# Third mixer of a hybrid encoder layer: the centring and the first chunk's right sides move into the two visits that complete the inverses, and merged values are turned eight blocks a visit

## Chip, cores and metric

The kernel runs on one core of a Trainium2 chip. The core has five engines with their own instruction queues: TensorE (PE in the profile; its weight loads are shown as PEld), VectorE (DVE), ScalarE (ACT), GpSimd (POOL) and SyncE (SP), which here only starts DMA transfers. The metric is the device time of one execution in microseconds; the median of the runs counts.

## What is computed

One encoder layer with a sequence of 256 tokens and a width of 2048. Three mixers read one normalised projection of the input, a gate is put on each, and an output product and an MLP follow:

```python
proj = u @ w_in                                   # u: RMS norm of x
y_a = stick_breaking_attention(...)               # first mixer
y_b = forgetting_attention(...)                   # second mixer
y_c = rwkv7_time_mix(rw, ...)                     # third mixer, 16 heads of 64
m = g_a * (y_a @ w_branch_a) + g_b * (y_b @ w_branch_b) + g_c * (y_c @ w_branch_c)
x = x + rms_norm(m @ w_out)
x = x + rms_norm(jnp.square(relu(rms_norm(x) @ w_mlp_up)) @ w_mlp_down)
```

The third mixer is a recurrence over time with a 64 by 64 state for each head:

```python
sa = jnp.einsum('bhvk,bhk->bhv', state, kk_t)
state = state * w_t[:, :, None, :] - sa[..., None] * kka_t[:, :, None, :] + v_t[..., None] * k_t[:, :, None, :]
y = jnp.einsum('bhvk,bhk->bhv', state, r_t)
```

Then each head's output has its mean taken away, is divided by its deviation and scaled (a group norm), and is gated.

## The kernel before

**The stream of weights.** Nearly all of the time goes to large products of activations with weights read once from memory, each element kept as a rounded high part and a low part. `wraw` (L162) issues a DMA of 512 KB from SyncE into one of three `raw` buffers. `wsplit` (L170) makes the high part `whi` on ScalarE (L173) and the low part `wlo` on VectorE (L175), each in one of three buffers. TensorE then multiplies with both, in `gemm` (L187, matmuls at L191, L195 and L197) or in `tok` (L208, matmuls at L220 and L235). These are the large matmuls in what follows, of 512 or 256 columns. A step of `tok` is one such weight tile: eight large matmuls with `whi`, then four with `wlo`.

**The mixers beside it.** The mixers are a generator. `tick` (L137) is called at fixed places of the stream, twice a step of the stream as a rule; it adds a credit of 0.88 (`SHARE`) times a weight and runs pieces of the generator as long as there is credit and no hold. A piece ends with a `yield`: a plain number costs that much credit, and `("stage", cost, hold)` also holds the generator back for that many ticks. So small matmuls of the mixers come between the large ones in groups; such a group is called a visit here. A list `hooks` is served at each tick too, one entry a tick.

**What sets the order.** From L436 on, only TensorE's instructions stand in the order in which the code writes them (`manual_schedule(engines={PE})`). VectorE's and ScalarE's order is made by a list scheduler with its own estimate of when operands are ready. A change that only moves matmuls therefore also moves instructions of VectorE and ScalarE.

**The third mixer, one half of the heads at a time** (`rwkv_half`, run for half 0 and half 1). Time is cut in four chunks of 64. For each of four pairs of heads, matmuls at L836 make the products of keys within the chunks, and VectorE masks them into SC. Then comes the part that the change touches:

- Centring: 16 matmuls at L857 take the mean over a head away from the values `v`, by a constant matrix "cen", into two PSUM tiles; 8 ScalarE copies (L862) put them into four tiles Xt. This is a visit of its own, ahead of the inverse.
- The inverse: VectorE transposes SC to U (L876) and inverts 64 triangular blocks of 32 by 32 in 31 steps (L881 and L883, tiles tp and Ti). Then it transposes the inverses Ti to TW (L888) and back into SC (L893).
- Two visits complete the inverses of the 64 by 64 blocks: 32 matmuls at L898 with TW, copied back to TW by ScalarE (L900), and 32 at L905, copied to SC (L908).
- For each chunk c: right sides at L928 (from chunk 1 on also L924), copied by ScalarE to `rh` (L932); the solution at L937, copied to Xt (L941, L943); then the outputs and the next state (L949, L955, L958).

**Merged values.** After each gate and branch product, the sum `m` of the gated branches, 256 tokens by 512 columns, is turned by `turn`: each call makes four transposes of 128 by 128 on TensorE (L1112) and splits the result into two tiles `pk` (ScalarE L259, VectorE L260). Six of these calls, for the first three groups of columns, are hooks during the fourth group's branch product of the third mixer.

Of the kernel before, what the change touches and what calls it, by code (L numbers as in the profile page):

```python
# [11 lines left out]
F32 = mybir.dt.float32  # L12
F32R = mybir.dt.float32r
AF = mybir.ActivationFunctionType
ALU = mybir.AluOpType
AX = mybir.AxisListType
# [36 lines left out]
def hybrid_block(ctx, tc, xt, x, gains, params, consts, lora, gup, wst, out):  # L53
    nc = tc.nc
    V, A, G, PE = nc.vector, nc.scalar, nc.gpsimd, nc.tensor
# [10 lines left out]
    def nm(s):  # L66
        uid[0] += 1
        return f"{s}_{uid[0]}"
# [4 lines left out]
    def mps():  # L73
        return pm.tile([128, 512], F32, tag="mps", name=nm("mps"), bufs=4)
# [11 lines left out]
    def C(name, r=slice(0, 128), lo=0, hi=None):  # L86
        c0, w = CC[name]
        hi = w if hi is None else hi
        if name == "ident":
            return ident[r, lo:hi]  # L90
        if c0 < NR + 128:
            return cr[r, c0 - 128 + lo:c0 - 128 + hi].bitcast(F32)
        return con[r, c0 - 128 - NR + lo:c0 - 128 - NR + hi]
# [13 lines left out]
    done = {}  # L107
# [6 lines left out]
    each, hooks = [], []  # L114
# [610 lines left out]
    def rwkv_half(hf):  # L725
# [26 lines left out]
        pss = []  # L752
# [97 lines left out]
            V.tensor_tensor(bon[p], psb[:, 0:T], v, ALU.mult)  # L850
            yield ("stage", 1.9, 3.5 if i == 0 else 2.0)

        pss = [mps(), mps()]
        for i, p in enumerate(PR):
            for cc in range(4):
                o = 256 * (i % 2) + 128 * (cc // 2)
                PE.matmul(pss[i // 2][64 * (cc % 2):64 * (cc % 2) + 64, o:o + 128], done[f"v{p}"][:, cc * 64:cc * 64 + 64],  # L857
                          C("cen"), start=True, stop=True)
        for i, p in enumerate(PR):
            Xt[p] = rp.tile([128, 4, 128], F32, tag="AX", name=nm("Xt"), bufs=5)  # L860
            for b in range(2):
                A.activation(Xt[p][64:128, b:4:2, :],  # L862
                             pss[i // 2][64 * b:64 * b + 64, 256 * (i % 2):256 * (i % 2) + 256]
                             .rearrange("p (c t) -> p c t", c=2), AF.Copy)
        yield ("stage", 0.2, 1)

        U = rp.tile([64, 32, 32], F32, tag="b6", name=nm("U"), bufs=1)
        Ti = rp.tile([64, 32, 32], F32, tag="Ti", name=nm("Ti"), bufs=1)
        tp = rp.tile([64, T], F32, tag="kkr", name=nm("tp"), bufs=1)
# [27 lines left out]
        for j in range(32):  # L897
            PE.matmul(ps[32 * (j % 4):32 * (j % 4) + 32, j // 4 * 32:j // 4 * 32 + 32], SC[0:32, j, 32:64],  # L898
                      TW[0:32, j, :], start=True, stop=True)
        for g in range(4):  # L900
            A.activation(TW[32:64, g:32:4, :], ps[32 * g:32 * g + 32, 0:256].rearrange("p (a b) -> p a b", a=8), AF.Copy)
        yield ("stage", 0.2, 3)
        ps = mps()
        for j in range(32):
            PE.matmul(ps[32 * (j % 4):32 * (j % 4) + 32, j // 4 * 32:j // 4 * 32 + 32], TW[32:64, j, :],  # L905
                      SC[32:64, j, 32:64], start=True, stop=True)
        for g in range(4):
            A.activation(SC[0:32, g:32:4, 32:64], ps[32 * g:32 * g + 32, 0:256].rearrange("p (a b) -> p a b", a=8),  # L908
                         AF.Copy)
        yield ("stage", 0.2, 2)  # L910


        Pb = rp.tile([128, 4, 128], F32, tag="Pb", name=nm("Pb"), bufs=1)
        G.memset(Pb, 0.0)
        y = {p: g1() for p in PR}
        HC = (slice(0, 64), slice(64, 128))
        for c in range(4):
            sls = [[i * 8 + h * 4 + c for h in range(2)] for i in range(4)]
            co = [slice(64 * i, 64 * i + 64) for i in range(4)]
            psr = mps()  # L920
            if c:
                for i, p in enumerate(PR):
                    for hc in HC:
                        PE.matmul(psr[hc, co[i]], Bt[p][:, c, 0:64], Pb[:, i, hc], start=i == 0, stop=False,  # L924
                                  skip_group_check=True)
            for i, p in enumerate(PR):
                for h, hc in enumerate(HC):
                    PE.matmul(psr[hc, co[i]], SC[64:128, sls[i][h], 0:64], Xt[p][64:128, c, hc],  # L928
                              start=c == 0 and i == 0, stop=True, skip_group_check=True)
            rhs = rp.tile([64, 4, 128], F32, tag="rh", name=nm("rh"), bufs=1)  # L930
            for hc in HC:
                A.activation(rhs[:, :, hc], psr[hc, 0:T].rearrange("p (a b) -> p a b", a=4), AF.Copy)  # L932
            yield ("stage", 0.9, 1)
            pso = [mps(), mps()]
            for i in range(4):
                for h, hc in enumerate(HC):
# [170 lines left out]
    def turn(g, j):  # L1107
        ps = mps()
        for i in range(2):
            for tt in range(2):  # L1110
                c = 256 * i + 128 * tt
                PE.transpose(ps[:, c:c + 128], ms[g][:, tt, (j + i) * 128:(j + i) * 128 + 128], C("ident"))  # L1112
        for i in range(2):
            mpk[4 * g + j + i] = pk()
            split(ps[:, T * i:T * i + T], mpk[4 * g + j + i], 0.5)

    for g in range(4):
        if g == 3:
            hooks.extend([lambda: None] * 12)
            for k in range(0, 12, 2):  # L1120
                hooks.extend([lambda k=k: turn(k // 4, k % 4), lambda: None])
        branch(ycp, thc.pop(0) if thc else gate(), ms[g], False)
    hooks.extend([lambda: None] * 4 + [lambda: turn(3, 0), lambda: None, lambda: turn(3, 2)])
    wo = tok(mpk)
# [587 lines left out]
```

## Time and profile before

| | us |
|---|---|
| median of three runs (1503.62, 1504.09, 1506.31) | 1504.09 |
| the profiled execution | 1505.64 |
| its span, first to last instruction | 1503.8 |
| TensorE busy | 1489.7 (99%) |
| TensorE weight loads busy | 1250.7 (83%) |
| VectorE busy | 1206.8 (80%) |
| ScalarE busy | 938.4 (62%) |
| GpSimd busy | 91.1 (6%) |
| mean granted TensorE clock | 0.998 |

A row of a timeline is: start, length, engine, line, operation, output and inputs by the program's tile names, their shape, and how many equal instructions in a row are put together. Where an engine stood idle ahead of it, the idle time and what ended it stand in brackets. TensorE's matmuls overlap: a row's length is from the start of its first to the modelled end of its last, so times are compared from start to start. A small matmul of the mixers shows as two in the trace: the 16 of the centring read x32, the 32 at L898 x64 and the 8 right sides of a chunk x16.

### The profile page before, as it was taken

The numbers are of one execution on the slowest core, as the hardware profiler recorded it, in microseconds if no ns is written. First come the engines' busy times: TensorE is split into PE (matmuls) and PEld (weight loads), VectorE is DVE, ScalarE is ACT, GpSimd is POOL, SyncE is SP. The second block draws the span as 40 slices with busy tenths as digits, with TensorE's granted clock in tenths as the row PEclk, the third lists the DMA queues.
The fourth block names the chain that finished last, engine by engine and source line by source line (L and its number), as shares of the span: only waits on it lengthen the run. The fifth ranks groups of instructions, "written<-read, shape, count | busy, mean of one in ns | idle before, by whom it ended". The sixth has DMA issues, their size and how long they took to land.

```text
span 1503.8 us, 22719 instructions
## 1 busy us (share of the span) xinstructions
PE 1489.7 (99%) x8384; PEld 1250.7 (83%) x8384; DVE 1206.8 (80%) x1677; ACT 938.4 (62%) x1435; POOL 91.1 (6%) x151
## 2 busy tenths in 40 slices
PE   9999999999999999999999999999999999999997
PEld 7888888887788887788888888888888888888886
DVE  7965679895688796476657788999899989999996
ACT  7665677545776445564445776776767666767663
POOL 0011003000001000000000000000000000000000
PEclk9999999999999999999999999999999999999999
DMA  8545445454445455345674768879888888889874
GB/s 284 202 150 178 151 158 169 155 182 162 157 167 173 150 192 189 135 165 195 226 243 161 261 179 256 252 223 286 243 269 239 225 279 258 249 259 261 256 216 149
DMA packets 107055, 312.19 MB, mean 208 GB/s; under 512 B 12352, under 2 KB 14400, under 8 KB 106944
## 3 DMA queue, kind: packets, MB, share of 16 engines
q1 hardware_dynamic: 96336, 279.35, 54.8%
q0 software_dynamic: 8064, 29.36, 10.5%
q10 hardware_dynamic: 2544, 2.03, 0.5%
q8 instruction: 66, 1.08, 0.3%
q14 instruction: 45, 0.37, 0.1%
HBM read 279.24 MB, written 2.10 MB: 187 GB/s over the span
## 4 chain that ended last, share of the span: by engine, by line
PE 94%; DVE 2%; ACT 1%; issue 1%; DMA 0%; SPq 0%; POOLq 0%; DVEq 0%; POOL 0%; ACTq 0%
PE gps L235 27%; PE gps L191 22%; PE gps L195 12%; PE gps L220 7%; PE mps L1430 3%; PE mps L1432 3%; PE mps L1431 3%; PE gps L1432 2%; PE gps L1430 2%; PE gps L1431 2%; PE gps L197 2%; DVE wlo L175 1%; PE mps L836 1%; PE gps L359 1%; PE gps L1219 1%
## 5 line engine op out<-in xcount | busy, mean ns | idle before, releaser
L175 DVE TENSOR_TENSOR wlo<-raw,whi 128x1024 fp32r<-128x1024 f32 x570 | 691.3, 1223 | 151.5 <-ACT whi L173 141.8
L173 ACT ACTIVATE whi<-raw 128x1024 fp32r<-128x1024 f32 x570 | 597.9, 1057 | 246.5 <-PE gps L235 71.7
L191 PE MATMUL gps<-pk,whi 128*128 128x512 f32 x1460 | 370.7, 392 | 1.0 <-ACT whi L173 0.8
L191 PEld LDWEIGHTS gps<-pk,whi 128*128 128x128 f32 x1460 | 270.6, 188 | 56.4 <-ACT whi L173 1.7
L235 PE MATMUL gps<-whi,pk 128*128 128x512 f32 x1004 | 253.5, 392 | 0.0
L195 PEld LDWEIGHTS gps<-pk,wlo 128*128 128x128 f32 x1561 | 212.8, 190 | 15.4 <-DVE wlo L175 0.5
L235 PEld LDWEIGHTS gps<-whi,pk 128*128 128x128 f32 x1004 | 186.4, 188 | 40.0 <-issue 1.0
L195 PE MATMUL gps<-pk,wlo 128*128 128x256 f32 x1561 | 218.0, 282 | 0.1
L235 PE MATMUL gps<-wlo,pk 128*128 128x512 f32 x502 | 138.1, 393 | 0.1
L235 PEld LDWEIGHTS gps<-wlo,pk 128*128 128x128 f32 x502 | 93.1, 188 | 20.0 <-DVE wlo L175 0.5
L1347 ACT ACTIVATE tmp<-gps 128x256 f32<-128x256 f32 x64 | 24.6, 385 | 105.2 <-PE gps L197 103.3
L1430 PE MATMUL mps<-whi,fm 128*128 128x512 f32 x224 | 88.6, 396 | 1.4 <-ACT whi L173 1.3
L1431 PE MATMUL mps<-whi,fm 128*128 128x512 f32 x224 | 87.7, 392 | 0.0
L1432 PE MATMUL mps<-wlo,fm 128*128 128x512 f32 x224 | 87.4, 390 | 0.0
L1410 POOL DMA_DIRECT2D raw<-raw x56 | 48.8, 872 | 571.9 <-DVE raw L1407 279.8
L1407 DVE TENSOR_TENSOR raw<-raw,raw 128x1024 f32<-128x1024 f32 x56 | 68.4, 1222 | 0.8
L1430 PE MATMUL gps<-whi,fm 128*128 128x512 f32 x168 | 65.8, 392 | 0.0
L1432 PE MATMUL gps<-wlo,fm 128*128 128x512 f32 x168 | 65.7, 391 | 0.0
L1431 PE MATMUL gps<-whi,fm 128*128 128x512 f32 x168 | 65.5, 390 | 0.0
L220 PE MATMUL gps<-whi,pk 128*128 128x512 f32 x224 | 60.8, 393 | 0.0
L1430 PEld LDWEIGHTS mps<-whi,fm 128*128 128x128 f32 x224 | 42.3, 189 | 9.7 <-ACT whi L173 3.5
L1432 PEld LDWEIGHTS mps<-wlo,fm 128*128 128x128 f32 x224 | 42.1, 188 | 9.4
(358 smaller groups left out, 1743.0 us busy)
## 6 DMA issues: line engine op xcount, KB each, us to landing
raw<-in_wst_dram SPq DMA_DIRECT2D x510, 512.0 KB, 4.3
raw<-raw POOLq DMA_DIRECT2D x56, 512.0 KB, 7.2
x<-in_xt_dram SPq DMA_DIRECT2D x8, 256.0 KB, 5.6
x<-in_x_dram SPq DMA_DIRECT2D x8, 256.0 KB, 5.5
raw<-in_wst_dram SPq DMA_DIRECT2D x6, 256.0 KB, 4.9
pk<-in_wst_dram SPq DMA_DIRECT2D x6, 256.0 KB, 5.1
g<-in_gains_dram SPq DMA_DIRECT2D x4, 256.0 KB, 5.0
pk<-in_gains_dram SPq DMA_DIRECT2D x4, 256.0 KB, 6.8
```

The costliest lines, as they stand in the source:

```text
L173: A.activation(hi, raw, AF.Copy)
L175: low = lambda: V.tensor_tensor(lo, raw, hi.bitcast(F32), ALU.subtract)
L191: PE.matmul(ps, hi[:, i * 128:i * 128 + 128], pks[i], start=first and i == 0, stop=False)
L195: PE.matmul(ps[:, 0:T], lo[:, i * 128:i * 128 + 128], pks[i][:, 0:T], start=False, stop=False)
L197: PE.matmul(ps, hi[:, (n - 1) * 128:n * 128], pks[n - 1], start=False, stop=True)
L220: PE.matmul(ps[tt], pks[k][:, c:c + 128], w[:, (k - k0) * 512:(k - k0) * 512 + 512], start=k == 0 and part == 0 and w is hl[0], stop=w is ...
L235: PE.matmul(ps[tt], pks[k][:, c:c + 128], w[:, (k - k0) * 512:(k - k0) * 512 + 512], start=k == 0 and part == 0 and w is hl[0], stop=False)
L1407: V.tensor_tensor(R[d, a], R[d, a], R[d, b], ALU.add)
L1410: G.dma_start(out=R[d, a], in_=R[d, b], accum_op=ALU.add)
L1430: PE.matmul(Q[f], a, w, start=d == d0 and i == 0, stop=False)
L1431: PE.matmul(Q[f], b, w, start=False, stop=False)
L1432: PE.matmul(Q[f], a, wl, start=False, stop=d == dn and i == 1)
```

## The change

In `rwkv_half` the centring visit ahead of the inverse is removed. Its 16 matmuls now follow the 32 at L898 in the first of the two completing visits, and its copies to Xt follow ScalarE's copies to TW, in two parts. The right sides of chunk 0 (L928 with c = 0) now follow the 32 matmuls of the second completing visit (L905), and the copy to `rh` follows the copies to SC. Holds and credits are divided anew, with the same sum of holds. The transposes of merged values in the hooks come as three entries of eight transposes, four ticks apart, in place of six entries of four, two ticks apart. No instruction is added or removed on any engine.

```diff
@@ -850,20 +850,6 @@
             V.tensor_tensor(bon[p], psb[:, 0:T], v, ALU.mult)
             yield ("stage", 1.9, 3.5 if i == 0 else 2.0)
 
-        pss = [mps(), mps()]
-        for i, p in enumerate(PR):
-            for cc in range(4):
-                o = 256 * (i % 2) + 128 * (cc // 2)
-                PE.matmul(pss[i // 2][64 * (cc % 2):64 * (cc % 2) + 64, o:o + 128], done[f"v{p}"][:, cc * 64:cc * 64 + 64],
-                          C("cen"), start=True, stop=True)
-        for i, p in enumerate(PR):
-            Xt[p] = rp.tile([128, 4, 128], F32, tag="AX", name=nm("Xt"), bufs=5)
-            for b in range(2):
-                A.activation(Xt[p][64:128, b:4:2, :],
-                             pss[i // 2][64 * b:64 * b + 64, 256 * (i % 2):256 * (i % 2) + 256]
-                             .rearrange("p (c t) -> p c t", c=2), AF.Copy)
-        yield ("stage", 0.2, 1)
-
         U = rp.tile([64, 32, 32], F32, tag="b6", name=nm("U"), bufs=1)
         Ti = rp.tile([64, 32, 32], F32, tag="Ti", name=nm("Ti"), bufs=1)
         tp = rp.tile([64, T], F32, tag="kkr", name=nm("tp"), bufs=1)
@@ -897,40 +883,60 @@
         for j in range(32):
             PE.matmul(ps[32 * (j % 4):32 * (j % 4) + 32, j // 4 * 32:j // 4 * 32 + 32], SC[0:32, j, 32:64],
                       TW[0:32, j, :], start=True, stop=True)
+        pss = [mps(), mps()]
+        for i, p in enumerate(PR):
+            for cc in range(4):
+                o = 256 * (i % 2) + 128 * (cc // 2)
+                PE.matmul(pss[i // 2][64 * (cc % 2):64 * (cc % 2) + 64, o:o + 128], done[f"v{p}"][:, cc * 64:cc * 64 + 64],
+                          C("cen"), start=True, stop=True)
         for g in range(4):
             A.activation(TW[32:64, g:32:4, :], ps[32 * g:32 * g + 32, 0:256].rearrange("p (a b) -> p a b", a=8), AF.Copy)
-        yield ("stage", 0.2, 3)
+        yield ("stage", 0.1, 1.5)
+        for i, p in enumerate(PR):
+            Xt[p] = rp.tile([128, 4, 128], F32, tag="AX", name=nm("Xt"), bufs=5)
+            if i == 2:
+                yield ("stage", 0.1, 1.5)
+            for b in range(2):
+                A.activation(Xt[p][64:128, b:4:2, :],
+                             pss[i // 2][64 * b:64 * b + 64, 256 * (i % 2):256 * (i % 2) + 256]
+                             .rearrange("p (c t) -> p c t", c=2), AF.Copy)
+        yield ("stage", 0.2, 2)
         ps = mps()
         for j in range(32):
             PE.matmul(ps[32 * (j % 4):32 * (j % 4) + 32, j // 4 * 32:j // 4 * 32 + 32], TW[32:64, j, :],
                       SC[32:64, j, 32:64], start=True, stop=True)
+        HC = (slice(0, 64), slice(64, 128))
+        co = [slice(64 * i, 64 * i + 64) for i in range(4)]
+        psr = mps()
+        for i, p in enumerate(PR):
+            for h, hc in enumerate(HC):
+                PE.matmul(psr[hc, co[i]], SC[64:128, i * 8 + h * 4, 0:64], Xt[p][64:128, 0, hc], start=i == 0,
+                          stop=True, skip_group_check=True)
         for g in range(4):
             A.activation(SC[0:32, g:32:4, 32:64], ps[32 * g:32 * g + 32, 0:256].rearrange("p (a b) -> p a b", a=8),
                          AF.Copy)
-        yield ("stage", 0.2, 2)
+        yield 0.2
 
 
         Pb = rp.tile([128, 4, 128], F32, tag="Pb", name=nm("Pb"), bufs=1)
         G.memset(Pb, 0.0)
         y = {p: g1() for p in PR}
-        HC = (slice(0, 64), slice(64, 128))
         for c in range(4):
             sls = [[i * 8 + h * 4 + c for h in range(2)] for i in range(4)]
-            co = [slice(64 * i, 64 * i + 64) for i in range(4)]
-            psr = mps()
             if c:
+                psr = mps()
                 for i, p in enumerate(PR):
                     for hc in HC:
                         PE.matmul(psr[hc, co[i]], Bt[p][:, c, 0:64], Pb[:, i, hc], start=i == 0, stop=False,
                                   skip_group_check=True)
-            for i, p in enumerate(PR):
-                for h, hc in enumerate(HC):
-                    PE.matmul(psr[hc, co[i]], SC[64:128, sls[i][h], 0:64], Xt[p][64:128, c, hc],
-                              start=c == 0 and i == 0, stop=True, skip_group_check=True)
+                for i, p in enumerate(PR):
+                    for h, hc in enumerate(HC):
+                        PE.matmul(psr[hc, co[i]], SC[64:128, sls[i][h], 0:64], Xt[p][64:128, c, hc],
+                                  start=False, stop=True, skip_group_check=True)
             rhs = rp.tile([64, 4, 128], F32, tag="rh", name=nm("rh"), bufs=1)
             for hc in HC:
                 A.activation(rhs[:, :, hc], psr[hc, 0:T].rearrange("p (a b) -> p a b", a=4), AF.Copy)
-            yield ("stage", 0.9, 1)
+            yield ("stage", 0.9, 1 if c else 2)
             pso = [mps(), mps()]
             for i in range(4):
                 for h, hc in enumerate(HC):
@@ -1117,8 +1123,8 @@
     for g in range(4):
         if g == 3:
             hooks.extend([lambda: None] * 12)
-            for k in range(0, 12, 2):
-                hooks.extend([lambda k=k: turn(k // 4, k % 4), lambda: None])
+            for k in range(3):
+                hooks.extend([lambda k=k: [turn(k, 0), turn(k, 2)]] + [lambda: None] * 3)
         branch(ycp, thc.pop(0) if thc else gate(), ms[g], False)
     hooks.extend([lambda: None] * 4 + [lambda: turn(3, 0), lambda: None, lambda: turn(3, 2)])
     wo = tok(mpk)
```

TensorE's order around the first completing visit of the first half, before (the L898 matmuls read TW; `whi` and `wlo` are the parts of a weight tile, with its number):

```order
L235 MATMUL gps_3470<-wlo_3533,pk_332 128x512
L235 MATMUL gps_3471<-wlo_3533,pk_332 128x512
L235 MATMUL gps_3470<-wlo_3533,pk_333 128x512
L235 MATMUL gps_3471<-wlo_3533,pk_333 128x512
L898 MATMUL mps_3566<-TW_3447,SC_2240 32x32 x32
L235 MATMUL gps_3470<-whi_3550,pk_334 128x512 x2
```

and after, where these matmuls are at L884 and the centring is at L890:

```order
L235 MATMUL gps_3440<-wlo_3503,pk_332 128x512
L235 MATMUL gps_3441<-wlo_3503,pk_332 128x512
L884 MATMUL mps_3534<-TW_3405,SC_2240 32x32 x32
L890 MATMUL mps_3567<-con,g_448_2349 64x128 x4
L890 MATMUL mps_3567<-con,g_468_2427 64x128 x4
L890 MATMUL mps_3568<-con,g_480_2486 64x128 x4
L890 MATMUL mps_3568<-con,g_497_2564 64x128 x4
L235 MATMUL gps_3440<-wlo_3503,pk_333 128x512
```

The visit stands two large matmuls earlier in the stream, and the centring follows in it. The second completing visit and the right sides of chunk 0 were two visits, at L905 and L928, with one step of the stream between them; after, they are one:

```order
L220 MATMUL gps_3441<-wlo_3619,pk_338 128x512
L220 MATMUL gps_3441<-wlo_3619,pk_339 128x512
L906 MATMUL mps_3659<-SC_2240,TW_3405 32x32 x32
L913 MATMUL mps_3692<-Xt_3607,SC_2240 64x64 x2
L913 MATMUL mps_3692<-Xt_3610,SC_2240 64x64 x2
L913 MATMUL mps_3692<-Xt_3613,SC_2240 64x64 x2
L913 MATMUL mps_3692<-Xt_3634,SC_2240 64x64 x2
L235 MATMUL gps_3716<-whi_3641,pk_1346 128x512 x2
```

It stands where the right sides stood, twelve large matmuls behind the place of L905. VectorE's order at the end of the inverse of the first half, before:

```order
L881 TENSOR_TENSOR tp_3042<-U_3040,Ti_3041 64x31
L883 TENSOR_TENSOR Ti_3041<-Ti_3041,tp_3042 64x31
L175 TENSOR_TENSOR wlo_3533<-raw_3530,whi_3532 128x1024
L888 STREAM_TRANSPOSE TW_3447<-Ti_3041 32x16x32 x2
L893 STREAM_TRANSPOSE SC_2240<-Ti_3041 32x16x32 x2
L175 TENSOR_TENSOR wlo_3551<-raw_3548,whi_3550 128x1024
```

and after (L881, L883, L888 and L893 are now L867, L869, L874 and L879):

```order
L867 TENSOR_TENSOR tp_3002<-U_3000,Ti_3001 64x31
L869 TENSOR_TENSOR Ti_3001<-Ti_3001,tp_3002 64x31
L175 TENSOR_TENSOR wlo_3521<-raw_3518,whi_3520 128x1024
L874 STREAM_TRANSPOSE TW_3405<-Ti_3001 32x16x32 x2
L879 STREAM_TRANSPOSE SC_2240<-Ti_3001 32x16x32 x2
L175 TENSOR_TENSOR wlo_3594<-raw_3591,whi_3593 128x1024
```

The rows look alike, but the `wlo` ahead of TW is now that of the step behind the visit (before it was that of the step just ahead of it): all are one step further on. In the second half, before:

```order
L888 STREAM_TRANSPOSE TW_5736<-Ti_5353 32x16x32 x2
L175 TENSOR_TENSOR wlo_5729<-raw_5726,whi_5728 128x1024
L893 STREAM_TRANSPOSE SC_4615<-Ti_5353 32x16x32 x2
L175 TENSOR_TENSOR wlo_5750<-raw_5747,whi_5749 128x1024
L175 TENSOR_TENSOR wlo_5776<-raw_5773,whi_5775 128x1024
```

and after:

```order
L874 STREAM_TRANSPOSE TW_5696<-Ti_5315 32x16x32 x2
L175 TENSOR_TENSOR wlo_5720<-raw_5717,whi_5719 128x1024
L879 STREAM_TRANSPOSE SC_4615<-Ti_5315 32x16x32 x2
L175 TENSOR_TENSOR wlo_5746<-raw_5743,whi_5745 128x1024
L175 TENSOR_TENSOR wlo_5765<-raw_5762,whi_5764 128x1024
```

There too every `wlo` stands one place earlier relative to the transposes: wlo_5729, wlo_5750 and wlo_5776 of before are, by the step of the stream that uses them, wlo_5701 (ahead of the last steps of the inverse), wlo_5720 and wlo_5746 of after.

## The prediction, made before the changed kernel was run

> **What bounds the kernel now.** I read the busy shares first, then tables by stretches, then the timeline of TensorE and of VectorE at the places that the diff touches.
>
> ```profile
> PE 1489.7 (99%) x8384; PEld 1250.7 (83%) x8384; DVE 1206.8 (80%) x1677; ACT 938.4 (62%) x1435; POOL 91.1 (6%) x151
> 279.40:295.00 15.60, 15.60 (x110) 13.46 (x109) 14.99 (x31) 10.05 (x18) 0.20 (x2) 1.00 0.31 102
> ...
> 315.00:335.20 20.20, 20.20 (x136) 16.85 (x136) 19.75 (x39) 9.25 (x14) 0.10 (x1) 1.00 0.55 183
> 513.00:545.00 32.00, 32.00 (x166) 26.39 (x165) 31.03 (x58) 15.86 (x22) 0.00 (x0) 1.00 0.45 150
> 545.00:568.00 23.00, 23.00 (x102) 18.77 (x101) 22.47 (x44) 10.14 (x13) 0.00 (x0) 1.00 0.54 182
> ...
> 1480.00:1504.00 24.00, 14.05 (x63) 11.29 (x61) 14.09 (x25) 5.38 (x12) 1.46 (x2) 0.85 0.35 110
> ```
>
> In the rows by stretch the columns are the stretch, its length, then PE, weight load, VectorE, ScalarE and GpSimd busy, the granted clock, DMA share and GB/s. TensorE is busy 99% of the span and all of the first four stretches, so time goes there only where TensorE's row of work gets longer or a wait appears. The second fact is less plain: these four are the two inverses (L881/L883), and there VectorE is busy 14.99 of 15.60 and 19.75 of 20.20, and in the second half 31.03 of 32.00 and 22.47 of 23.00. It makes the inverse and every `wlo` (L175) that TensorE eats. Both engines are full together. Work of TensorE that stands in such a stretch is cover for VectorE, and the 16 centring matmuls stand right at its head.
>
> **What a visit costs.** Rows of TensorE at the visits concerned, first half:
>
> ```profile
> 280.65 0.84 PE L191 MATMUL gps<-pk,whi 128*128 128x512 f32 x3
> 281.43 1.97 PE L857 MATMUL mps<-con,g 128*64 128x128 f32 x32
> 283.32 0.73 PE L191 MATMUL gps<-pk,whi 128*128 128x512 f32 x2
> ...
> 333.87 1.07 PE L235 MATMUL gps<-wlo,pk 128*128 128x512 f32 x4
> 334.87 0.75 PE L898 MATMUL mps<-TW,SC 32*32 32x32 f32 x64
> 335.55 1.20 PE L235 MATMUL gps<-whi,pk 128*128 128x512 f32 x4
> ...
> 344.30 0.61 PE L220 MATMUL gps<-wlo,pk 128*128 128x512 f32 x2
> 344.84 0.68 PE L928 MATMUL mps<-Xt,SC 64*64 64x64 f32 x16
> 345.45 2.11 PE L235 MATMUL gps<-whi,pk 128*128 128x512 f32 x8
> 347.40 0.61 PE L235 MATMUL gps<-wlo,pk 128*128 128x512 f32 x2
> 348.03 1.08 PE L937 MATMUL mps<-rh,SC 64*64 64x64 f32 x16
> ```
>
> Starts are what counts. Four large matmuls take 1.07 with a last one of 0.39, so they start 0.227 apart. The last large one before L898 starts at 333.87+1.07-0.39 = 334.55, the next at 335.55; less one pitch that is 0.77, and the row behind is 0.13 longer than its like (1.20 against 1.07), of which I count 0.11: 0.88 us for the visit, 0.75-0.19 = 0.56 of it the matmuls and 0.32 the switch. The same working gives centring 283.32-281.10-0.23+0.11 = 2.10 (1.70 + 0.40) and L928 345.45-344.52-0.23+0.11 = 0.81 (0.46 + 0.35). L905 has the row of L898 again, 0.88.
>
> **Merging visits.** Two visits in one lose one switch (0.32) and gain a junction between two kinds of matmul. Its price shows where kinds already follow each other:
>
> ```profile
> 276.70 1.16 PE L836 MATMUL mps<-Bt,At 64*128 64x128 f32 x16
> 277.79 0.66 PE L840 MATMUL mps<-ident,At 128*128 128x128 f32 x4
> ...
> 354.65 0.69 PE L924 MATMUL mps<-Pb,Bt 128*64 128x64 f32 x16
> 355.27 0.68 PE L928 MATMUL mps<-Xt,SC 64*64 64x64 f32 x16
> ```
>
> Last L836 start 276.70+1.16-0.27 = 277.59, then 277.79: 0.20. Last L924 start 355.12, then 355.27: 0.15. I take 0.175, so a merge saves 0.145; four merges (two in each half) 0.6 us, with 0 and 1.28 (a free junction) as ends. The Trainium skill, "TensorE: Matmul & The Clock Gate", section "Part 3: Packing small matmuls — row/col tiling", says that a weight load overlaps matmuls in flight only when its row group differs; taken strictly every junction here would cost a full switch and the merges nothing, 0.6 us more in the sum. The rows 0.20 and 0.15 against 0.32 speak for about half.
>
> The third edit, eight transposes a visit in place of four, removes three switches:
>
> ```profile
> 703.71 1.07 PE L235 MATMUL gps<-whi,pk 128*128 128x512 f32 x4
> 704.62 0.60 PE L1112 MATMUL mps<-ident,m 128*128 128x128 f32 x4
> 704.97 1.18 PE L235 MATMUL gps<-whi,pk 128*128 128x512 f32 x4
> ```
>
> The last large matmul before them starts at 703.71+1.07-0.39 = 704.39, so the transposes start 0.23 behind, one plain pitch, and are left 0.35 later, with 0.11 behind. They are 128 rows by 128 like the stream and pay hardly any switch: I take 0, ends -0.3 and +0.3. ScalarE and VectorE then split four blocks in a row, some 4 x 0.43 = 1.7 us on each by the row of such a split further down (L257); 18 and 14 large matmuls (3.2 us at least) stand between one turn and the next, and the product that reads the blocks begins behind the transposes of 735.
>
> **What the moved centring uncovers, first half.** VectorE's rows ahead of the first visit of the inverse's end:
>
> ```profile
> 329.77 1.23 DVE L175 TENSOR_TENSOR wlo<-raw,whi 128x1024 fp32r<-128x1024 f32 x1
> 330.91 2.25 DVE L888 STREAM_TRANSPOSE TW<-Ti 32x512 f32<-32x512 f32 x2
> 333.06 2.12 DVE L893 STREAM_TRANSPOSE SC<-Ti 32x512 f32<-32x512 f32 x2
> 335.21 1.23 DVE L175 TENSOR_TENSOR wlo<-raw,whi 128x1024 fp32r<-128x1024 f32 x1
> ```
>
> L898 reads TW, which is ready at 330.91+2.25 = 333.16; the visit starts at 334.87, so 1.71 us are to spare. Without 2.10 us of centring ahead, and with the visit two large matmuls earlier (0.45), TensorE arrives at 332.32. VectorE doesn't come earlier: from 279.4 to here its timeline has no row with a wait, so I let nothing in it shrink. The new order also puts the `wlo` that stood behind the SC transposes (335.21) ahead of TW, 330.91-329.77 = 1.14 us more: TW at 334.30. TensorE waits about 2.1 us, and starts the visit at 334.4. That is the place of before: 334.4+0.45 = 334.85 against 334.87. The centring that was removed in front bought nothing, and its matmuls now lie behind this point, on the path.
>
> From there: before 0.88+0.88+0.81 = 2.57 for three visits; after, first visit 0.56+0.175+1.70+0.40 = 2.84 and second 0.56+0.175+0.46+0.35 = 1.55, in all 4.39. So +1.82. One gain: L937 follows ten large matmuls behind L928 and waits for `rh` (start 0.09 late, and the 16 take 1.08 where L928's 16 take 0.68): 0.49 us. It now has 18 matmuls of cover, and that goes. First half: -0.02+1.82-0.49 = **+1.3**.
>
> **Second half.** The same stretch, where the scheduler had already put one `wlo` between the transposes:
>
> ```profile
> 563.14 2.32 DVE L888 STREAM_TRANSPOSE TW<-Ti 32x512 f32<-32x512 f32 x2
> 565.38 1.17 DVE L175 TENSOR_TENSOR wlo<-raw,whi 128x1024 fp32r<-128x1024 f32 x1
> 566.48 2.20 DVE L893 STREAM_TRANSPOSE SC<-Ti 32x512 f32<-32x512 f32 x2
> 568.71 2.36 DVE L175 TENSOR_TENSOR wlo<-raw,whi 128x1024 fp32r<-128x1024 f32 x2
> 565.80 0.84 PE L220 MATMUL gps<-whi,pk 128*128 128x512 f32 x3
> 566.60 0.73 PE L220 MATMUL gps<-wlo,pk 128*128 128x512 f32 x2
> 570.37 1.07 PE L235 MATMUL gps<-wlo,pk 128*128 128x512 f32 x4
> 572.18 0.62 PE L220 MATMUL gps<-wlo,pk 128*128 128x512 f32 x2
> 579.07 0.75 PE L898 MATMUL mps<-TW,SC 32*32 32x32 f32 x64
> ```
>
> Here the visit (579.07) is far behind the transposes (568.68), and the `wlo`s are what TensorE meets. The one of 565.38 is ready at 566.55 and used at 566.60, 0.23 us late (start 0.35 behind the last one instead of 0.227, and 0.73 for 0.62). The two of 568.71 are ready at 569.9 and 571.07, used at 570.37 and 572.18. With 2.10+0.23 gone these uses come at 564.27, 568.04 and 569.85. In the new order each `wlo` stands one place earlier: the first where its forerunner was, ahead of the last steps of the inverse (ready near 562.5), the second between TW and SC (566.55+1.14 = 567.7, as one more is ahead of TW); both in time, the second by 0.35. Only the third stays behind SC, at 571.07 since VectorE has the same work up to it. TensorE waits 1.2 there (ends: 0 if VectorE were faster, 2.33 if the new order brings nothing). Then +1.82 as above, no `rh` wait to gain: -2.33+1.2+1.82 = **+0.7**.
>
> **What else moves.**
>
> ```profile
> 282.57 3.10 ACT L862 ACTIVATE Xt<-mps 64x256 f32<-64x256 f32 x8
> ```
>
> ScalarE's 8 copies to Xt (L862, issued next to centring before) now follow the four to TW, 3.10 us in all by the row below; 38 large matmuls (8.6 us) lie between the two visits, so they are hidden, at a cost of up to 1 us if that cover fell. Queues of SP and POOL keep their order; the weight DMAs follow TensorE through three buffers and shift with it. Should TensorE's wait of 2.1 us lower the clock, the price would be some 0.8 us: the last 24 us, with 9.95 idle, were granted 0.85. I take 0, as 1.00 was granted everywhere in these stretches. The Trainium skill, same page, section "Part 1: The HAM clock gate (the "warmup" mystery)", puts the window at about 3.4 us of idling, which a 2.1 us wait would not fill; no run here shows it yet.
>
> **Sum.** +1.3 +0.7 = +2.0 us, the merges' -0.6 inside it. The profiled execution took 1505.64, 1.55 over the median 1504.09 of the three runs; against the median the forecast is **1506.1 us**, 0.13% more. 0.2%, or 3.0 us, is about what a measurement can tell from no change.
>
> **Rivals.**
> - *The cover was not needed.* If TW came before 332.3 and the third `wlo` before 569.9, the change would give its merges (-0.6), the `rh` wait (-0.49) and the late `wlo` (-0.23): 1502.8. Against it: a VectorE without one wait for 54 us.
> - *The second half loses as much as the first.* VectorE decides: if the new order leaves that third `wlo` at 572.2 or later, 1.1 us more than forecast, TensorE gets all 2.33 back as wait and pays the whole 1.82: sum 1.3+1.82 = +3.1, 1507.2, just over the bound, and slower still with each `wlo` put ahead of a transposition (1.14). For it: 97% busy, and uses that I have within 0.4 us of being ready.
> - *The third mixer ends late.* Its last visits stand six large matmuls later (1.36 us), and its last values are split just ahead of the product that reads them:
>
> ```profile
> 663.85 0.43 DVE L257 TENSOR_TENSOR pk<-g,pk 128x256 fp32r<-128x256 f32 x1 [0.36 <-ACT pk L256]
> 668.35 1.07 PE L220 MATMUL gps<-whi,pk 128*128 128x512 f32 x4
> ```
>
> 4.07 us lie between; 1.36 of it go, and ScalarE and VectorE shift other work into the rest. If that fails by up to 1 us: 1507.1. Against it: 2.7 us left on paper.
> - *The clock drops* at the wait: 1506.9 or more.
>
> **Chances.** Forecast 0.50; second half in full 0.26; late end 0.12; cover not needed 0.08; clock 0.04. Slower by over 0.2% holds most of the second case and half of the two late ones, and the forecast's upper edge: 0.41. Faster by over 0.2% would need 1501.1, below even the first rival: 0.04. Within: 0.55. The range leaves out the first rival's lower part, and goes up to both upper rivals together (1508.3): 1503.2 to 1508.6.
>
> **What would show it.** Right: the first visit's L898 begins near 334.4 with about 2 us of idling ahead that TW's transposes end; the centring behind it starts about 0.2 behind the last of L898's; L943 waits for no `rh`; near 570 a `wlo` wait of about 1.2. Wrong: no wait at the first visit (then VectorE was not the bound), junctions of 0.3 (merges give nothing), a wait in L220 near 668, or TensorE idling in the turns at 704 to 717.

## The result: 0.12% slower, by a wait that the forecast has and a clock that it left out

The changed kernel takes 1506.51 us (median of 21 runs, 1504.97 to 1509.34), the kernel before 1504.39 (21 runs, 1503.41 to 1508.96). The ratio is 1.0012, with a 95% interval of 1.0006 to 1.0017. That is slower, by less than the 0.2% that the prediction calls no change, and close to the 1506.1 forecast.

The spans of the two profiled executions say the opposite, and are no evidence: 1503.2 after against 1503.8 before. Two places that the change doesn't touch make that difference. The start up to the last L836 visit of the first half took 275.87 after and 276.70 before. And from the last transposes of merged values to the end it was 767.4 after and 768.6 before; there the execution of before has waits in the MLP that the other doesn't have (TensorE's timeline of before):

```profile
1199.74 0.50 PE L1430 MATMUL mps<-whi,fm 128*128 128x512 f32 x1 [0.66 <-ACT whi L173]
1200.72 2.11 PE L191 MATMUL gps<-pk,whi 128*128 128x512 f32 x8 [0.25 <-DVE tmp L1348]
```

So I compare the stretch that the change touches, between visits that stand at the same place of the stream in every kernel: the last L836 visit of the first half, the second visit of the first half's group norm (L100), the last L836 visit of the second half, the first turn, and the last one. TensorE's rows of these, before (the first of them, 276.70, is in the prediction) and after:

```profile
408.45 0.39 PE L100 MATMUL mps<-hl,cr 128*128 128x512 f32 x1
509.92 1.16 PE L836 MATMUL mps<-Bt,At 64*128 64x128 f32 x16
704.62 0.60 PE L1112 MATMUL mps<-ident,m 128*128 128x128 f32 x4
735.20 0.60 PE L1112 MATMUL mps<-ident,m 128*128 128x128 f32 x4
```

```profile
275.87 1.16 PE L836 MATMUL mps<-Bt,At 64*128 64x128 f32 x16
408.38 0.39 PE L100 MATMUL mps<-hl,cr 128*128 128x512 f32 x1
509.81 1.16 PE L836 MATMUL mps<-Bt,At 64*128 64x128 f32 x16
705.44 1.03 PE L1118 MATMUL mps<-ident,m 128*128 128x128 f32 x8
735.79 0.60 PE L1118 MATMUL mps<-ident,m 128*128 128x128 f32 x4
```

The first half took 131.75 and now 132.51, the second 194.70 and now 195.63, the turns 30.58 and now 30.35: +0.76, +0.93 and -0.23; from the first visit to the last it is +1.42 (459.92 against 458.50).

**First half, after.** TensorE's rows, then VectorE's:

```profile
330.94 0.61 PE L235 MATMUL gps<-wlo,pk 128*128 128x512 f32 x2
333.04 0.75 PE L884 MATMUL mps<-TW,SC 32*32 32x32 f32 x64 [1.48 <-DVE TW L874]
333.72 1.97 PE L890 MATMUL mps<-con,g 128*64 128x128 f32 x32
335.62 0.74 PE L235 MATMUL gps<-wlo,pk 128*128 128x512 f32 x2
...
344.50 0.75 PE L906 MATMUL mps<-SC,TW 32*32 32x32 f32 x64
345.18 0.68 PE L913 MATMUL mps<-Xt,SC 64*64 64x64 f32 x16
...
350.14 0.68 PE L943 MATMUL mps<-rh,SC 64*64 64x64 f32 x16
```

```profile
329.76 1.23 DVE L175 TENSOR_TENSOR wlo<-raw,whi 128x1024 fp32r<-128x1024 f32 x1
330.91 2.08 DVE L874 STREAM_TRANSPOSE TW<-Ti 32x512 f32<-32x512 f32 x2
332.90 2.10 DVE L879 STREAM_TRANSPOSE SC<-Ti 32x512 f32<-32x512 f32 x2
```

TensorE arrives, idles 1.48 us for TW (L874), and begins the visit at 333.04, 0.05 behind the end of TW's transposes (332.99). The centring that was cover ahead of the inverse is now behind this point. L943 takes 0.68 where L937 took 1.08: the wait for `rh` is gone.

**Second half, after.** TensorE's row of the wait and VectorE's rows that it waits for:

```profile
568.80 1.08 PE L220 MATMUL gps<-whi,pk 128*128 128x512 f32 x4
571.07 0.73 PE L220 MATMUL gps<-wlo,pk 128*128 128x512 f32 x2 [1.19 <-DVE wlo L175]
```

```profile
564.29 2.27 DVE L874 STREAM_TRANSPOSE TW<-Ti 32x512 f32<-32x512 f32 x2
566.46 1.17 DVE L175 TENSOR_TENSOR wlo<-raw,whi 128x1024 fp32r<-128x1024 f32 x1
567.56 2.20 DVE L879 STREAM_TRANSPOSE SC<-Ti 32x512 f32<-32x512 f32 x2
569.79 3.69 DVE L175 TENSOR_TENSOR wlo<-raw,whi 128x1024 fp32r<-128x1024 f32 x3
```

Two `wlo`s come in time and the one behind the SC transposes (ready near 571) is 1.19 us late.

### The profile page after: what moved, and what is told of

Same layout as the page of the kernel before. It is cut to its first block, busy times and chain, and to the rows that moved or that the text cites. A ratio compares the mean times of both kernels' runs of the same rounds, so it can differ in the third digit from the quotient of the medians.

```text
span 1503.2 us, 22717 instructions
## 1 busy us (share of the span) xinstructions
PE 1487.7 (99%) x8384; PEld 1250.8 (83%) x8384; DVE 1206.5 (80%) x1677; ACT 938.5 (62%) x1435; POOL 91.1 (6%) x151
## 3 DMA queue, kind: packets, MB, share of 16 engines
q8 instruction: 66, 1.08, 0.3%
## 4 chain that ended last, share of the span: by engine, by line
PE 91%; DVE 5%; issue 2%; ACT 1%; DMA 0%; DVEq 0%; POOLq 0%; POOL 0%; SPq 0%; ACTq 0%
PE gps L235 26%; PE gps L191 21%; PE gps L195 11%; PE gps L220 7%; PE mps L1436 3%; PE mps L1437 3%; PE mps L1438 3%; PE gps L1436 2%; PE gps L1438 2%; PE gps L1437 2%; DVE wlo L175 2%; PE gps L197 1%; PE gps L359 1%; DVE Ti L869 1%; DVE tp L867 1%
```

## The experiments

Theory: at the head of the inverse the centring was cover for a VectorE that sets the pace there. Its removal comes back as waits for VectorE, and behind the inverse it lies on TensorE's path. Rivals: the loss is in the merged right sides or in the turns, or in an order of ScalarE and VectorE that has nothing to do with their load.

All kernels were timed beside the kernel before. Its median was 1504.39 beside the first row of the table, and 1504.15, 1504.82 and 1504.61 beside the three groups of runs that the other rows come from. The table gives the ratio, and from each one's profile the change against before of the three stretches above, worked out from the starts of the same visits as there.

| kernel | median us | ratio, 95% interval | first half | second half | turns | 276 to 735 |
|---|---|---|---|---|---|---|
| whole change | 1506.51 | 1.0012, 1.0006 to 1.0017 | +0.76 | +0.93 | -0.23 | +1.4 |
| the same, second | 1508.21 | 1.0019, 1.0011 to 1.0028 | +2.37 | +0.98 | -0.23 | +3.1 |
| the same, third | 1507.32 | 1.0016, 1.0007 to 1.0024 | +2.45 | +0.99 | -0.23 | +3.2 |
| centring alone | 1507.31 | 1.0017, 1.0006 to 1.0028 | +2.57 | +1.14 | 0.00 | +3.7 |
| right sides alone | 1504.26 | 0.9993, 0.9983 to 1.0002 | -0.65 | -0.24 | 0.00 | -0.9 |
| turns alone | 1504.87 | 1.0000, 0.9990 to 1.0010 | -0.30 | -0.08 | -0.23 | -0.7 |
| right sides and turns | 1503.76 | 0.9994, 0.9984 to 1.0004 | -0.70 | -0.26 | -0.24 | -1.2 |
| the same, second | 1503.63 | 0.9990, 0.9981 to 0.9998 | -0.66 | -0.19 | -0.23 | -1.1 |
| centring first in its visit | 1505.57 | 1.0002, 0.9993 to 1.0011 | -0.15 | +1.00 | -0.23 | +0.6 |
| light inverse, before | 1505.55 | 1.0007, 0.9998 to 1.0016 | +0.41 | +0.09 | 0.00 | +0.5 |
| light inverse, whole change | 1504.26 | 0.9995, 0.9986 to 1.0004 | -0.32 | -0.58 | -0.23 | -1.2 |
| longer wait | 1510.13 | 1.0034, 1.0022 to 1.0046 | +5.54 | +0.96 | -0.23 | +6.2 |
| shorter wait | 1504.86 | 0.9999, 0.9991 to 1.0008 | -0.83 | +0.94 | -0.23 | -0.1 |

### The centring alone

The centring's matmuls leave their place ahead of U and come behind those of L898, and its copies to Xt behind those to TW, as in the change:

```diff
-        pss = [mps(), mps()]
-        for i, p in enumerate(PR):
-            for cc in range(4):
...
-        yield ("stage", 0.2, 1)
...
+        pss = [mps(), mps()]
+        for i, p in enumerate(PR):
+            for cc in range(4):
...
-        yield ("stage", 0.2, 3)
+        yield ("stage", 0.1, 1.5)
...
+        yield ("stage", 0.2, 1)
```

> Only the centring is moved: it follows the L898 matmuls in the first completing visit of each half; the right sides of chunk 0 stay a visit of their own and the turns stay in fours. Theory (cover): the centring at the head of the inverse ran while VectorE was the limit, so taking it away there is given back as waits for VectorE, and behind the inverse it lies on TensorE's path. First half: -2.1 for the removed visit, some 1.5 to 1.7 of waiting for TW at the first completing visit, +1.9 for the insertion, so +1.3; second half -2.1 -0.25, a wlo wait near 571 of about 1.4, +1.9, so +1.0. Together about +2.4 us against before (ratio 1.0015), more than the whole change. Rival (the move is a saving of two visits and the loss lies in the merged right sides or the turns): -0.4 us and no wait at the first completing visit.

Measured: 1.0017, +3.7 us in the stretch, all of the loss and more. The theory's part stands: the waits are there, 1.55 us for TW and 1.22 us for the `wlo` of the second half (the last row below). But the first half lost 2.57 instead of 1.3. The row of the centring shows where:

```profile
333.24 0.75 PE L884 MATMUL mps<-TW,SC 32*32 32x32 f32 x64 [1.55 <-DVE TW L874]
333.92 2.69 PE L890 MATMUL mps<-con,g 128*64 128x128 f32 x32
336.55 1.22 PE L235 MATMUL gps<-wlo,pk 128*128 128x512 f32 x2
337.56 2.40 PE L235 MATMUL gps<-whi,pk 128*128 128x512 f32 x8
...
573.01 0.73 PE L220 MATMUL gps<-wlo,pk 128*128 128x512 f32 x2 [1.22 <-DVE wlo L175]
```

The same 32 matmuls that take 1.97 in the first trace of the change take 2.69 here, and the large ones behind them are slow too. This was a second price that I had not expected, and it is followed up below.

### The right sides alone, the turns alone, both together

The right sides of chunk 0 behind the matmuls of L905, with a hold of 3 so that L937 keeps its place in the stream:

```diff
+        psr = mps()
+        for i, p in enumerate(PR):
+            for h, hc in enumerate(HC):
+                PE.matmul(psr[hc, co[i]], SC[64:128, i * 8 + h * 4, 0:64], Xt[p][64:128, 0, hc], start=i == 0,
+                          stop=True, skip_group_check=True)
...
-            yield ("stage", 0.9, 1)
+            yield ("stage", 0.9, 1 if c else 3)
```

> Only the right sides of chunk 0 go into the second completing visit, with the hold behind them such that L937's place in the stream is that of before; the centring stays ahead of the inverse, the turns in fours. Theory: one switch less in each half (-0.2 each) and no wait for rh at the first L937 of the first half (-0.5): about -0.9 us (ratio 0.9994). Rival (the loss of the whole change sits here, since ScalarE's copies to SC and rh now queue behind one visit): +1 us or more, with a wait for rh or SC on TensorE behind the visit.

The turns:

```diff
-            for k in range(0, 12, 2):
-                hooks.extend([lambda k=k: turn(k // 4, k % 4), lambda: None])
+            for k in range(3):
+                hooks.extend([lambda k=k: [turn(k, 0), turn(k, 2)]] + [lambda: None] * 3)
```

> Only the merged values are turned eight blocks a visit. Theory: the transposes have the shape of the stream and pay hardly any switch, so three visits fewer give 0.1 to 0.2 us; ratio 0.9999, no difference that a measurement tells. Rival: the longer burst of splits on ScalarE and VectorE makes a whi or wlo late between 704 and 720: +0.5 us or more, seen as idle time of TensorE there.

The third kernel has both edits.

> The right sides of chunk 0 and the turns of the change, with the centring left where it was: the change without the part that the theory blames. Theory: -0.9 and -0.15, about -1.0 us (ratio 0.9993), so faster than both before and the whole change (by some 2.5 us against the latter). Rival (the parts only help or hurt together): between before and the whole change.

> The change without the moved centring a second time, to tell a difference of 1 us from none: -0.9 to -1.2 us against before (ratio 0.9993) in the stretch from 279 to 740 and in the median; rival: no difference (1.0000).

Measured: right sides -0.9 us in the stretch, as expected, and a ratio of 0.9993 whose interval still reaches 1.0002. Turns alone: -0.23 us in the turns; its ratio of 1.0000 tells nothing, and its -0.30 in the first half is the wait at L937, shorter in that execution (16 matmuls in 0.88 instead of 1.08, with TensorE's order unchanged); it isn't counted for the turns. In the execution of before a `whi` ahead of the copies to `rh` waited 1.19 us for its weights' DMA, and in this one it did not. No wait of TensorE appeared in the turns. Both together: 0.9994 and, a second time, 0.9990 (0.9981 to 0.9998); -1.2 and -1.1 us in the stretch in both traces. The change without the moved centring is, if anything, a little faster than the kernel before; the second interval leaves 1 out, the first one doesn't. Against the whole change it is some 3 to 4 us faster. No rival that puts the loss in these parts is left.

### The centring ahead of L898 in the same visit

Against the whole change:

```diff
-        ps = mps()
-        for j in range(32):
-            PE.matmul(ps[32 * (j % 4):32 * (j % 4) + 32, j // 4 * 32:j // 4 * 32 + 32], SC[0:32, j, 32:64],
-                      TW[0:32, j, :], start=True, stop=True)
         pss = [mps(), mps()]
...
+        ps = mps()
+        for j in range(32):
+            PE.matmul(ps[32 * (j % 4):32 * (j % 4) + 32, j // 4 * 32:j // 4 * 32 + 32], SC[0:32, j, 32:64],
+                      TW[0:32, j, :], start=True, stop=True)
```

> The whole change, but in the first completing visit the centring matmuls stand ahead of the L898 matmuls instead of behind them. They don't read TW, so TensorE can do them while it would wait. Theory (TensorE waits there for TW alone): the wait of about 1.5 us at the first completing visit of the first half goes, less a rest of 0 to 0.3; nothing changes in the second half, where no wait stands at that visit. About -1.5 us against the whole change, so -0.1 to +0.6 us against before (ratio 1.0000 to 1.0004). Rival (the wait is not TW's, or it comes back at the next wlo): no difference from the whole change, ratio 1.0012.

Measured: 1.0002, as the theory has it. TensorE's rows:

```profile
331.59 1.97 PE L886 MATMUL mps<-con,g 128*64 128x128 f32 x32
333.49 0.75 PE L890 MATMUL mps<-TW,SC 32*32 32x32 f32 x64
```

The centring fills the time in which TensorE would wait, L898's matmuls (here L890) start without a wait, and the first half goes from between +0.76 and +2.45 to -0.15. The second half keeps its +1.00, since its wait stands at the `wlo` near 570 and not at the visit.

Most of what keeps the first half at -0.15, above the -0.83 of the kernel without a wait further below, is a new stall at the first state update. TensorE's row and VectorE's:

```profile
350.92 1.27 PE L961 MATMUL mps<-Xt,Kt 128*64 128x64 f32 x15
350.65 0.97 DVE L947 COPY Xt<-mps 64x64 f32<-64x64 f32 x4
```

Up to this visit TensorE keeps the same distances as in the kernel without a wait. Here VectorE's copies to Xt end near 351.6, after the visit has begun; from its start to that of most of the L964 matmuls it takes 1.11 us (350.92 to 352.03), where the whole change takes 0.51 (352.35 to 352.86). That the copies are the cause is read from the rows, not tested.

### A lighter inverse

```diff
-            V.tensor_tensor(t3, U[:, s + 1:32, s:s + 1].to_broadcast([64, n, m]),
-                            Ti[:, s:s + 1, 0:m].to_broadcast([64, n, m]), ALU.mult)
-            V.tensor_tensor(Ti[:, s + 1:32, 0:m], Ti[:, s + 1:32, 0:m], t3, ALU.add)
+            if s < 21:
+                V.tensor_tensor(t3, U[:, s + 1:32, s:s + 1].to_broadcast([64, n, m]),
+                                Ti[:, s:s + 1, 0:m].to_broadcast([64, n, m]), ALU.mult)
+                V.tensor_tensor(Ti[:, s + 1:32, 0:m], Ti[:, s + 1:32, 0:m], t3, ALU.add)
```

> The kernel before, with the last 10 of the 31 steps of the inverse (L881 and L883, 20 small VectorE instructions in each half) left out, so VectorE has some 5 us less to do ahead of TW; TensorE's order is unchanged. The inverse is not complete, so the output is another one. Theory: VectorE's late wlo near 566 (0.23 us) goes; otherwise TensorE was not waiting: -0.2 us against before. Rival (TensorE's pace is set by VectorE in the kernel before too): -2 us or more.

> The whole change with the same 10 steps of the inverse left out. Theory (cover): with VectorE ahead, the centring visit at the head covers nothing, its removal is kept, and the waits at the first completing visit and near 571 are gone; what is left of the change are its merges and the rh wait: -1.0 to -1.5 us against the light kernel before, in place of about +2 for the change itself. Rival (the loss has nothing to do with VectorE's load): +1.5 to +2 us against the light kernel before, as with the full inverse.

Measured: the light kernel before takes 1505.55, the light whole change 1504.26, 1.3 us less; in the stretch -1.6 us (-1.2 against +0.5). With VectorE ahead the change gains; with the full inverse it loses. That is what the theory says, and a loss that has nothing to do with VectorE's load would have stayed. At the first completing visit no wait is left (TensorE's row in the light whole change):

```profile
331.42 0.75 PE L885 MATMUL mps<-TW,SC 32*32 32x32 f32 x64
```

The light kernel before isn't 0.2 us faster than the full one, as I had expected, but 0.5 slower in the stretch: the scheduler had moved other work, and a `whi` came late:

```profile
326.26 2.11 PE L235 MATMUL gps<-whi,pk 128*128 128x512 f32 x8 [0.58 <-ACT whi L173]
```

So some 0.4 of the 1.6 us is not the change's own: this wait of 0.58, against one of 0.20 for a `wlo` at 325.31 in the light whole change.

### The wait longer, shorter, and a third time

In the first half alone the wait was lengthened by one VectorE addition ahead of TW's transposes, and taken away by leaving out both instructions of the last two steps of the inverse. Both edits are against the whole change:

```diff
+        if hf == 0:
+            V.tensor_tensor(TW[0:32], Ti[0:32], Ti[0:32], ALU.add)
```

```diff
+            if hf or s < 29:
```

> The whole change with one VectorE instruction added ahead of TW's transposes in the first half (an addition of Ti to itself into TW, 32 by 1024, which the transposes overwrite); the scheduler also puts one SC transpose ahead of TW with it, so TW comes some 2.3 us later and TensorE waits some 3.8 us at the first completing visit instead of 1.5. In two of three traces so far the granted clock fell to 0.50 behind that wait of 1.5, for some 3 us. Theory (the idling itself lowers the clock, the longer the surer): the drop is there, and the time is 2.3 us over the whole change plus what the drop costs (1.6 us) where the whole change had none: about +4.5 to +6 us against before (ratio 1.003 to 1.004). Rival (the drop has nothing to do with the wait): +2.3 us over the whole change, and the clock at 1.00 as often as not.

> The whole change with the last 2 of the 31 steps of the inverse left out in the first half alone (4 small VectorE instructions, about 1 us; the output is another one); the scheduler then also leaves the wlo behind TW's transposes, so TW comes some 2 us earlier. Theory: no wait at the first completing visit and no clock drop behind it, the second half as in the whole change: -1.6 us for the wait and another -1.6 where the drop was, so about 0 to +0.6 us against before (ratio 1.0002). Rival (the loss is the order behind the inverse, not the wait): +2 us as with the whole change.

The whole change was run twice more:

> The whole change once more, beside the three above: about +2 us against before (ratio 1.0012); its trace has the wait for TW at the first completing visit of the first half (about 1.5 us) and a wlo wait near 571 (about 1.2).

> The whole change a third time, for the spread: about +2 to +3 us against before. Its trace tells whether the granted clock falls behind the wait of 1.5 us at the first completing visit (one of the two traces of this kernel has it): with the drop the stretch from 279 to 740 is longer than before's by 3.0 us, without it by 1.4.

TensorE's rows in the third trace of the whole change, in that of the longer wait, and in that of the shorter one:

```profile
333.14 0.75 PE L884 MATMUL mps<-TW,SC 32*32 32x32 f32 x64 [1.56 <-DVE TW L874]
333.82 3.61 PE L890 MATMUL mps<-con,g 128*64 128x128 f32 x32
337.36 0.73 PE L235 MATMUL gps<-wlo,pk 128*128 128x512 f32 x2
```

```profile
335.10 1.08 PE L886 MATMUL mps<-TW,SC 32*32 32x32 f32 x64 [3.46 <-DVE TW L876]
336.11 3.68 PE L892 MATMUL mps<-con,g 128*64 128x128 f32 x32
339.72 1.22 PE L235 MATMUL gps<-wlo,pk 128*128 128x512 f32 x2
```

```profile
331.26 0.75 PE L885 MATMUL mps<-TW,SC 32*32 32x32 f32 x64
331.94 1.97 PE L891 MATMUL mps<-con,g 128*64 128x128 f32 x32
```

And the granted clock (third column from the right) of the 8 us around the visit, first trace of the whole change, third trace, longer wait:

```profile
331.00:339.00 8.00, 6.52 (x114) 5.27 (x113) 6.43 (x6) 3.57 (x9) 0.00 (x0) 1.00 0.51 163
```

```profile
331.00:339.00 8.00, 6.44 (x106) 5.45 (x105) 6.12 (x7) 3.43 (x8) 0.00 (x0) 0.79 0.56 169
```

```profile
331.00:339.00 8.00, 4.54 (x95) 4.02 (x95) 6.30 (x7) 3.39 (x8) 0.00 (x0) 0.73 0.39 117
339.00:343.00 4.00, 4.00 (x19) 3.05 (x16) 1.23 (x1) 2.19 (x6) 0.00 (x0) 0.68 0.30 114
```

Behind a wait of about 1.5 us the granted clock fell in three of four executions (second and third of the whole change, centring alone) and stayed at 1.00 in one. A clock of 0.79 over 8 us is 1.7 us of clock lost, and the first half is 1.6 to 1.7 us longer in the two executions of the whole change with the drop (+2.37, +2.45 against +0.76). With the wait of 3.46 us the drop was longer, 2.2 us lost in the first 8 us and 1.3 in the next 4. The ratio, 1.0034, is in the range expected; the +6.2 us in the stretch of its one trace is just above it. Without a wait at that visit (shorter wait, centring first, light whole change) the clock stayed at 1.00. In the kernel with the shorter wait the first half is as short as its merges and the `rh` wait make it: -0.83, where two merges at 0.20 and the wait of 0.49 add up to 0.89. Between 270 and 740 us none of the fourteen traces has a lower clock anywhere else. The rival, a drop that has nothing to do with the wait, has no execution for it.

## Why the prediction was right, point by point

- **What bounds.** VectorE in the two inverses: right. The light inverse turns the sign of the change.
- **The first half's wait**: right in place and cause, 2.1 us forecast and 1.48 to 1.56 measured. The term was mis-sized because I let nothing in VectorE shrink and counted the whole 1.14 for one more `wlo` ahead of TW: TW's transposes begin at 330.91 in both traces, while the execution of the change was 0.83 ahead at the last L836 visit (275.87 against 276.70). So they came 0.83 later and not 1.14, with one `wlo` more between U and TW as forecast (18 for 17), and they took 2.08 instead of 2.25. Why one more `wlo` cost only 0.83 stays open.
- **Merges**: a junction costs 0.12 (333.04+0.75-0.19 = 333.60 to 333.72, and 345.06 to 345.18) and not 0.175. A merge saves 0.20, four of them 0.8 us in place of 0.6. The strict reading of the Trainium skill, "TensorE: Matmul & The Clock Gate", section "Part 3: Packing small matmuls — row/col tiling", by which they would save nothing, doesn't hold here: 0.12 stands against a switch of 0.32. The forecast also applied that rule too widely. At the junction of L905 with the right sides the matmuls read partitions 32 to 63 and then 64 to 127, so their row groups do differ; at that of L898 with the centring they read 0 to 31 and then all 128, so their row groups overlap. Both junctions cost 0.12.
- **The `rh` wait** went, as forecast. Its size of 0.49 is that of one execution: with TensorE's order unchanged these 16 matmuls took 0.88 instead of 1.08 in the trace of the turns alone.
- **Second half**: +0.7 forecast, +0.93 to +0.99 measured. The `wlo` wait stands at 571.07, and the late `wlo` near 566 is gone. The idle time there is 1.19, but from start to start the wait costs 1.36 (571.07 less 568.80 and four pitches of 0.227), where I had 1.2. I also left out that the large matmuls behind a wait are slower (0.73 for 0.62 at 571.07, 1.09 for 1.07 next). These add 0.29, and the two cheaper junctions take back 0.11.
- **Turns**: 0 forecast with ends at 0.3, -0.23 measured.
- **The clock**: the step that failed. I took 0 and gave the drop 0.04, with a price of 0.8 us worked out from the last 24 us; it came in three of four executions with that wait and cost 1.6 to 1.7. I argued from a clock of 1.00 in stretches that had no wait in them, which says nothing of a stretch that has one.
- **The rivals**: "the cover was not needed" fell with the wait for TW. "The second half loses as much as the first" fell: the third `wlo` was ready near 571, not 572.2. "The third mixer ends late": between 600 and 705 no trace of the change has a wait on TensorE. "The clock drops" came true beside the forecast.

So the mechanism of the waits was right, and that the sum of 2.0 us came so close is in part luck, by errors that cancel: about 0.6 too much for waits, junctions and turns together (+1.4 in the execution without the drop), and nothing for a drop that adds 1.6 to 1.7 (+3.1 and +3.2 in the two with it). The median lies 2.1 us above before in the first set of runs, 3.4 and 2.7 in the other two.

## What to carry to other kernels

Where two engines are full at the same time, small work on the one is cover for the other; before moving it, look at the engine that will be waited for, not at the switches that the move saves. If the work doesn't need what the visit waits for, put it ahead of the waiting instruction: the same merge cost nothing in the first half with the centring first. And price a new wait on TensorE with its clock: here 1.5 us of idling cost some 3.1 in three of four executions.

## What the runs showed of the hardware

A wait of TensorE of 1.5 us can halve its granted clock. In three of four executions with waits of 1.48 to 1.56 us the clock fell to 0.50; the drop began 0.7 to 1.8 us behind the end of the wait and lasted 3.4 us. Here is the third trace of the whole change in three windows, of which the middle one is the drop:

```profile
333.40:333.80 0.40, 0.40 (x57) 0.38 (x43) 0.40 (x1) 0.00 (x0) 0.00 (x0) 1.00 0.68 277
333.80:337.20 3.40, 3.40 (x42) 3.28 (x32) 2.50 (x3) 1.57 (x3) 0.00 (x0) 0.50 0.33 103
337.20:337.60 0.40, 0.40 (x5) 0.24 (x2) 0.00 (x0) 0.38 (x2) 0.00 (x0) 0.97 0.77 118
```

In the trace of the longer wait the clock fell near 334.7, 0.4 us ahead of the wait's end, while no matmul ran, and came back near 341.5, 6.8 us later:

```profile
334.60:335.00 0.40, 0.00 (x0) 0.00 (x0) 0.40 (x1) 0.00 (x0) 0.00 (x0) 0.63 0.12 51
```

The Trainium skill, "TensorE: Matmul & The Clock Gate", section "Part 1: The HAM clock gate (the "warmup" mystery)", gives a free-running window of about 3.4 us: the lengths of the drops (3.4 us, and twice that behind the longer wait) and their changing distance from the wait agree with that. By the same section of the Trainium skill the clock goes down after at least one idle window of about 3.4 us; in the 3.4 us ahead of each of the three drops behind the shorter waits TensorE stood idle for only 1.51 to 1.56 us, so the traces disagree. The waits of 1.2 us near 571, which large matmuls follow, never lowered the clock (seven executions). Nor did small matmuls alone: where L898's and the centring's stand in one visit without a wait (shorter wait, centring first), it stayed at 1.00. Whether the waits of 1.2 us were harmless by their length, or whether the small matmuls behind the first half's wait add to its effect, was not tried, and why one execution with a wait of 1.48 us kept its clock is open.
